# Two transformer blocks on one core: last routing, norm rows, parameter tables and register loads changed together

## The chip, the cores and the metric

One Trainium2 chip, one of its cores. The metric is the device time of one execution in microseconds; the median of 3 runs of the kernel before is 1259.8 us (1259.2 to 1261.1). A profile was taken of one further execution.

## The reference, cut to what matters

Input x is 256 x 1024, float32. The first block is a norm, one projection, dilated attention beside a gated recurrence, an output projection, and 16 experts of which each takes 32 tokens (expert choice). The second block is a projection, three mixers, a layer norm (`ln1`), a router with 4 groups of 8 experts, and 32 small experts; each token goes to 2 experts of its best group; another layer norm (`ln2`) ends it:

```python
for l in range(DEPTH):
    h = hybrid_mixer(x, w_in[l], ...)
    x = layer_norm(DEEPNORM_ALPHA * x + h, ln1_w[l], ln1_b[l])
    h = hier_moe(x, router_group_w[l], router_group_b[l], router_expert_w[l], router_expert_b[l], ...)
    x = layer_norm(DEEPNORM_ALPHA * x + h, ln2_w[l], ln2_b[l])
```

The experts of the first block hold 192 MB of weights, those of the second 96 MB; each is read once.

## The kernel before, in words

**Stages.** `block1_mix` (first mixers), `moe1_route` and `moe1_experts` (first experts), the second block's mixers (`s5_mix`, `moba_mix`, `rwkv_mix`, `merge`), `mix_out` (output projection, layer norm, router logits), `moe2_route` and `moe2_experts` (second experts), `moe2_overflow` (a branch that is taken only when an expert has more tokens than its places), `finish` (last norm and stores). Rows of tokens come in two halves of 128, called a = 0 and 1.

**Order.** The engines take their instructions in order, each from its own queue; a planner fixes the order of each queue at build time from its own estimates, within the data dependences. `issue_after(ins)` adds a rule of order only: what the block emits on the engine of `ins` is queued behind `ins`. Loads are issued by SyncE (`nc.sync`), a few by ScalarE (`nc.scalar`) and GpSimd (`nc.gpsimd`); an issuing engine waits in its queue until the load's buffer is free.

**Weight loads of the second experts.** `prefetch2` issues loads of 1 MB in the order `ORDER2` (for each group of four experts gate and up of each, then the four downs; before the last group an extra set `E2` of weights, picked by a register that holds the number of the fullest expert, L1730). The buffers are a first-in first-out list `k.free2` of 18: six of `ringg`, five of `ey` and `x2p`, three of `ring`, one each of `X` (which holds x3 until then) and `cp2` (which holds the tables), two of `ringh`. A product that has used its weights appends their buffers to the list. Each of the 16 double steps of `moe2_experts` (L2002 gate and up of two experts, L2037 down of four) waits for its loads. In its last but one round of four experts, three buffers leave the list for good (`restore3`): two for norm rows, one for the rows `k.pre`.

**Routing.** `norm_rows` brings a half of x3 to SBUF, transposes it and takes the statistics; `logits` makes the router's 36 numbers per token; `split_rows` normalises the half (VectorE, L1637), and splits it into a high part (ScalarE, L1639, reading with a stride of 8 elements) and a low part (GpSimd, L1640). `route` (L1780 to L1789) picks the experts on VectorE in ten small operations; `moe2_route` counts places by a matmul (L1815, L1817), forms the one-hot `oh` of the first 8 experts (L1819), gathers their tokens by matmul (L1823) and evacuates them into `xi` (L1760 on ScalarE, L1762 on VectorE). `weights2` then makes the weights, the number of the fullest expert (`xid`) and the overflow flag (`over`, L1859); `onehot` makes the next octets' one-hots (L1959) and, on GpSimd, the weighted ones (L1961). `over` is loaded into a register of every engine (L1871).

**Norm rows and tables.** `load_norm` (L2102) reads each of the four vectors ln1_w, ln1_b, ln2_w, ln2_b from memory 128 times, into all partitions, on GpSimd's queue. `setup2` and `load_s5` load three parameter tables (L759, L760, L766) on ScalarE's queue between the first block's experts 3 and 4; `fold_router` (L1675 to L1687) uses them on GpSimd, then TensorE (L1683).

## Time and profile before

| | us |
|---|---|
| median of 3 runs | 1259.8 |
| profiled execution | 1256.34 |
| its span | 1254.6 |
| TensorE busy | 1039.7 |
| VectorE busy | 517.4 |
| ScalarE busy | 370.3 |
| GpSimd busy | 135.4 |

The span runs from the first to the last instruction of the profiled execution; the profiled execution's own time is slightly longer. PE is TensorE, PEld its weight loads, DVE VectorE, ACT ScalarE, POOL GpSimd, SP SyncE; SPq is SyncE's queue of instructions that issue loads. An engine's busy time does not say that it sets the end.

### The profile page before, as it was taken

The numbers are of one execution on the slowest core, as the hardware profiler recorded it, in microseconds if no ns is written. First come the engines' busy times: TensorE is split into PE (matmuls) and PEld (weight loads), VectorE is DVE, ScalarE is ACT, GpSimd is POOL, SyncE is SP. The second block draws the span as 40 slices with busy tenths as digits, with TensorE's granted clock in tenths as the row PEclk, the third lists the DMA queues.
The fourth block names the chain that finished last, engine by engine and source line by source line (L and its number), as shares of the span: only waits on it lengthen the run. The fifth ranks groups of instructions, "written<-read, shape, count | busy, mean of one in ns | idle before, by whom it ended". The sixth has DMA issues, their size and how long they took to land. (4 is left out here: it accounts for less than half of the span.)

```text
span 1254.6 us, 21023 instructions
## 1 busy us (share of the span) xinstructions
PE 1039.7 (83%) x8986; PEld 718.3 (57%) x8986; DVE 517.4 (41%) x1034; ACT 370.3 (30%) x634; POOL 135.4 (11%) x134
## 2 busy tenths in 40 slices
PE   8889997777668777767689999999999979666775
PEld 7889874344214233312169998898999855333332
DVE  5595653102374000124047564686638552111114
ACT  5445632100000000200034565843433532111112
POOL 1351000010060000000001100112002210004101
PEclk9999998988779889987899999998999989888778
DMA  9723579999999999999973342242146659999994
GB/s 365 288 83 116 203 289 365 379 402 407 421 420 421 420 421 420 421 420 421 420 303 133 135 168 101 101 168 103 61 178 248 261 227 419 421 420 420 419 421 165
DMA packets 52949, 375.58 MB, mean 299 GB/s; under 512 B 5874, under 2 KB 6130, under 8 KB 8051
## 3 DMA queue, kind: packets, MB, share of 16 engines
q1 hardware_dynamic: 51842, 370.09, 73.6%
q10 hardware_dynamic: 432, 2.00, 0.5%
q0 software_dynamic: 576, 2.10, 0.4%
q8 instruction: 72, 1.18, 0.4%
q14 instruction: 27, 0.21, 0.0%
HBM read 373.12 MB, written 1.05 MB: 298 GB/s over the span
## 5 line engine op out<-in xcount | busy, mean ns | idle before, releaser
L692 PE MATMUL mx<-w,xin 128*32 128x512 f32 x1024 | 180.6, 662 | 61.3 <-DMA w<-in_w_expert_up_dram 45.9
L776 DVE TENSOR_TENSOR wl<-w,wh 128x1024 fp32r<-128x1024 f32 x116 | 148.3, 1281 | 76.0 <-ACT wh L775 75.6
L775 ACT CAST wh<-w 128x1024 fp32r<-128x1024 f32 x118 | 123.3, 1048 | 112.9 <-PE pj L793 63.6
L793 PE MATMUL pj<-x,wh 128*128 128x256 f32 x800 | 152.4, 289 | 1.2 <-ACT wh L775 0.7
L692 PEld LDWEIGHTS mx<-w,xin 128*32 128x32 f32 x1024 | 37.0, 115 | 181.0 <-DMA w<-in_w_expert_up_dram 82.5
L793 PEld LDWEIGHTS pj<-x,wh 128*128 128x128 f32 x800 | 126.4, 193 | 5.1 <-issue 2.3
L793 PE MATMUL pj<-x,wl 128*128 128x256 f32 x400 | 114.7, 287 | 0.2
L2002 PE MATMUL mx<-w,xi 128*32 128x256 f32 x1024 | 76.6, 404 | 38.4 <-DMA w<-in_expert_w_gate_dram 36.0
L719 PE MATMUL mx<-w,hT 128*32 128x256 f32 x1024 | 81.5, 472 | 17.4 <-DMA w<-in_w_expert_down_dram 9.2
L704 ACT ACTIVATE sg<-mx,rsl 64x512 f32<-64x512 f32 x16 | 10.9, 682 | 239.4 <-PE mx L692 237.2
L793 PEld LDWEIGHTS pj<-x,wl 128*128 128x128 f32 x400 | 77.3, 193 | 1.1 <-DVE wl L776 0.6
L2002 PEld LDWEIGHTS mx<-w,xi 128*32 128x32 f32 x1024 | 36.6, 115 | 70.6 <-issue 48.0
L705 DVE SCALAR_TENSOR_TENSOR sg<-sg,rsl,mx 64x512 f32<-64x512 f32 x16 | 12.0, 749 | 145.5 <-ACT sg L704 145.4
L719 PEld LDWEIGHTS mx<-w,hT 128*32 128x32 f32 x1024 | 37.9, 132 | 54.1 <-issue 20.6
L727 DVE COPY ysb<-mx 32x256 f32<-32x256 f32 x32 | 13.5, 423 | 112.4 <-ACT ysb L727 112.4
L807 PE MATMUL pj<-wh,hT 128*128 128x256 f32 x320 | 57.6, 281 | 0.0
L727 ACT COPY ysb<-mx 32x256 f32<-32x256 f32 x32 | 11.6, 362 | 141.5 <-PE mx L719 134.3
L807 PEld LDWEIGHTS pj<-wh,hT 128*128 128x128 f32 x320 | 49.1, 189 | 1.0 <-ACT osq L447 0.3
L2037 PE MATMUL mx<-w,hT 128*32 128x512 f32 x264 | 44.9, 633 | 0.5 <-ACT hT L2017 0.5
L807 PE MATMUL pj<-wl,hT 128*128 128x256 f32 x160 | 44.7, 279 | 0.0
L1704 DVE TENSOR_TENSOR sg<-sg,mx 64x256 f32<-64x256 f32 (+1 forms) x17 | 7.2, 423 | 87.9 <-ACT sg L1703 87.9
L1545 PE MATMUL mx<-y,wh 128*128 128x256 f32 x192 | 36.2, 288 | 1.5 <-DVE y L825 1.3
(606 smaller groups left out, 1836.8 us busy)
## 6 DMA issues: line engine op xcount, KB each, us to landing
w<-in_w_expert_gate_dram SPq DMA_DIRECT2D x64, 1024.0 KB, 14.9
w<-in_w_expert_up_dram SPq DMA_DIRECT2D x64, 1024.0 KB, 13.2
w<-in_w_expert_down_dram SPq DMA_DIRECT2D x64, 1024.0 KB, 13.7
w<-in_w_in_dram SPq DMA_DIRECT2D x43, 1024.0 KB, 5.0
w<-in_expert_w_gate_dram SPq DMA_DIRECT2D x33, 1024.0 KB, 19.9
w<-in_expert_w_up_dram SPq DMA_DIRECT2D x33, 1024.0 KB, 19.8
w<-in_expert_w_down_dram SPq DMA_DIRECT2D x33, 1024.0 KB, 19.8
w<-in_w_out_dram SPq DMA_DIRECT2D x8, 1024.0 KB, 4.8
```

The source lines that it names most:

```text
L692: last = T.matmul(ps1[32 * i:32 * i + 32, :], x, w[:, kk, 512 * (i % 2):512 * (i % 2) + 512], start=(j + kk == 0), stop=(j == 3 and kk == 1))
L704: A.activation(sg, ps1[0:64, :], AF.Silu, scale=k.rsl[:, e:e + 1])
L705: V.scalar_tensor_tensor(sg, sg, k.rsl[:, e:e + 1], ps1[64:128, :], OP.mult, OP.mult)
L719: last = T.matmul(ps3[32 * q:32 * q + 32, 0:256], hT[:, ft % 4, (ft // 4) * 32:(ft // 4) * 32 + 32], d[:, kk, q * 256:(q + 1) * 256], star ...
L727: done = (V.tensor_copy if q % 2 else A.copy)(ysb[r0:r0 + 32, q * 256:(q + 1) * 256], ps3[32 * q:32 * q + 32, 0:256])
L775: k.halved = k.nc.scalar.copy(h, src).ins
L776: eng.tensor_tensor(l, src, h.bitcast(F32), OP.subtract)
L793: T.matmul(ps[:, m * S:(m + 1) * S], u[:, kk, :], v[:, kk, :], start=(kk + i == 0), stop=(kk == 7 and i == 2))
L807: T.matmul(ps[:, a * S:(a + 1) * S], u[:, 4 * kh + kk, a * P:(a + 1) * P], v[:, kk, :], start=(kh + a + kk + i == 0), stop=(kh + a == 2 an ...
L1545: T.matmul(pu[:, m * S:(m + 1) * S], u[:, kk, m * P:(m + 1) * P], v[:, kk, :], start=(kk + n == 0), stop=(kk == 3 and n == 2))
L2002: T.matmul(ps[64 * i + 32 * n:64 * i + 32 * n + 32, 0:256], x, ws[n][i][:, kk, :], start=(kk == 0), stop=(kk == 7))
L2037: T.matmul(py[q][32 * i:32 * i + 32, :], h[:, j, 32 * i:32 * i + 32], w[i][:, j, 512 * q:512 * q + 512], start=(j == 0), stop=(j == 1))
```

## The change

The three tables are issued on GpSimd's queue. `split_rows` writes the normalised half into a tile of its own, in the order that the split reads (VectorE for a = 0, ScalarE for a = 1); ScalarE copies the high part, VectorE takes the low part, for a = 1 behind the last pick. `route(1)` is emitted before `split_rows(1)`. Two counting products are queued behind the last gather on TensorE, `weights2` behind the last one-hot and the next octet's one-hot behind the last evacuation on VectorE. The two register loads are queued on SyncE behind the weight load emitted last before them. The norm vectors are loaded once as 4 rows (`load_norms`, one round of four experts earlier, where three buffers leave the list) and spread over the partitions by a product with a column of the identity and a copy by ScalarE (`spread_norm`).

```diff
--- before.py
+++ after.py
@@ -756,14 +756,14 @@
     n = k.s5o
     both = k.cp2.tile([P, n + k.io["cf2"].shape[1]], F32, tag="w0", bufs=1, name="p2")
     k.p2, k.c2f = both[:, 0:n], both[:, n:]
-    nc.scalar.dma_start(k.p2, k.io["p2"][:, 0:n])
-    nc.scalar.dma_start(k.c2f, k.io["cf2"])
+    nc.gpsimd.dma_start(k.p2, k.io["p2"][:, 0:n])
+    nc.gpsimd.dma_start(k.c2f, k.io["cf2"])
 
 
 def load_s5(k):
     n, m = k.s5o, k.io["p2"].shape[1]
     k.p2s = k.s5t.tile([P, m - n], F32, name="p2s")
-    k.nc.scalar.dma_start(k.p2s, k.io["p2"][:, n:m])
+    k.nc.gpsimd.dma_start(k.p2s, k.io["p2"][:, n:m])
 
 
 def split(k, src, eng=None):
@@ -1602,6 +1602,7 @@
     k.x3h = k.xg.tile([P, 2, D], F32R, name="x3h")
     k.x3l = k.xg.tile([P, 2, D], F32R, name="x3l")
     k.x3T = k.xg.tile([P, 8, S], F32, tag="xi2", bufs=2, name="x3T")
+    k.x3w = k.xg.tile([P, 2, D], F32, tag="xi2", bufs=2, name="x3w")
     k.lg = k.xg.tile([P, 2, 36], F32, name="lg")
     rw = k.p2v("rw").rearrange("p (k n) -> p k n", k=8)
 
@@ -1633,11 +1634,17 @@
         V.scalar_tensor_tensor(lg, lg, st[:, 4:5], k.rcs[:, 1], OP.mult, OP.add)
 
     def split_rows(a, st):
-        x = k.x3[:, a, :]
-        V.tensor_scalar(x, x, st[:, 1:2], st[:, 4:5], OP.add, OP.mult)
+        x, hi, lo = k.x3[:, a, :], k.x3h[:, a, :], k.x3l[:, a, :]
+        whole = k.x3w[:, a, :]
+        if a:
+            V.tensor_tensor(st[:, 7:8], st[:, 1:2], st[:, 4:5], OP.mult)
+            A.activation(by_row(whole), turned(x), AF.Identity, bias=st[:, 7:8], scale=st[:, 4:5])
+        else:
+            V.tensor_scalar(by_row(whole), turned(x), st[:, 1:2], st[:, 4:5], OP.add, OP.mult)
         with k.tc.issue_after(k.rows3.ins):
-            A.copy(by_row(k.x3h[:, a, :]), turned(x))
-        return G.tensor_tensor(by_row(k.x3l[:, a, :]), turned(x), by_row(k.x3h[:, a, :]).bitcast(F32), OP.subtract)
+            A.copy(hi, whole)
+        with k.tc.issue_after(k.picks2[a].ins) if a else nullcontext():
+            V.tensor_tensor(lo, whole, hi.bitcast(F32), OP.subtract)
 
     for m in range(8):
         if m == 4:
@@ -1657,13 +1664,13 @@
     out_rows(7, 1)
     logits(0, st[0])
     norm_rows(1, st[1])
+    route = route_rows(k)
     split_rows(0, st[0])
-    route = route_rows(k)
     route(0)
     with k.tc.issue_after(k.picks2[0].ins):
         logits(1, st[1])
+    route(1)
     split_rows(1, st[1])
-    route(1)
 
 
 def fold_router(k):
@@ -1727,10 +1734,11 @@
         src = k.io[f"expert_w_{name}_2"].rearrange("e (p k) n -> e p k n", p=P)
         if e == E2:
             if name == "gate":
-                k.more2 = k.nc.values_load(k.xid[0:1, 0:1], engines=(mybir.EngineType.SP,), min_val=0, max_val=E2 - 1)
+                with k.tc.issue_after(k.loads2.ins):
+                    k.more2 = k.nc.values_load(k.xid[0:1, 0:1], engines=(mybir.EngineType.SP,), min_val=0, max_val=E2 - 1)
             k.nc.sync.dma_start(t, src[bass.ds(k.more2, 1)].rearrange("e p k n -> p (e k) n"))
         else:
-            k.nc.sync.dma_start(t, src[e])
+            k.loads2 = k.nc.sync.dma_start(t, src[e])
 
 
 def loaded2(k, e, *names):
@@ -1759,7 +1767,7 @@
     if kk % 2:
         k.nc.scalar.activation(xi[:, kk, :], ps, AF.Identity, scale=w, bias=b)
     else:
-        k.nc.vector.tensor_scalar(xi[:, kk, :], ps, w, b, OP.mult, OP.add)
+        return k.nc.vector.tensor_scalar(xi[:, kk, :], ps, w, b, OP.mult, OP.add)
 
 
 def route_rows(k):
@@ -1816,18 +1824,19 @@
         if a:
             T.matmul(ps[:, 0:32], one, mk[:, 0, :], start=False, stop=True)
         V.tensor_tensor(k.pos[:, a], ps[:, 0:32], mk[:, a], OP.mult)
-        V.tensor_tensor(oh[:, a], io32(k), k.pos[:, a, 0:8, None].to_broadcast([P, 8, C2]), OP.is_equal)
+        k.last_oh = V.tensor_tensor(oh[:, a], io32(k), k.pos[:, a, 0:8, None].to_broadcast([P, 8, C2]), OP.is_equal)
         for kk in range(8):
             sl = slice((kk % 2) * 256, (kk % 2 + 1) * 256)
             for x in (k.x3h, k.x3l):
-                T.matmul(pg[kk // 2][:, sl], x[:, a, kk * P:(kk + 1) * P], oh[:, a].rearrange("p e c -> p (e c)"),
+                last = T.matmul(pg[kk // 2][:, sl], x[:, a, kk * P:(kk + 1) * P], oh[:, a].rearrange("p e c -> p (e c)"),
                          start=(a + kk % 2 == 0 and x is k.x3h), stop=(a == 1 and x is k.x3l), skip_group_check=True)
             if a:
-                gathered2(k, xi, kk, pg[kk // 2][:, sl])
+                k.last_xi = gathered2(k, xi, kk, pg[kk // 2][:, sl]) or k.last_xi
     k.wt2 = Wt.rearrange("p a g e -> p a (g e)")
     ps = k.pj()
-    T.matmul(ps[:, 0:32], one, mk[:, 0, :], start=True, stop=False)
-    T.matmul(ps[:, 0:32], one, mk[:, 1, :], start=False, stop=True)
+    with k.tc.issue_after(last.ins):
+        T.matmul(ps[:, 0:32], one, mk[:, 0, :], start=True, stop=False)
+        T.matmul(ps[:, 0:32], one, mk[:, 1, :], start=False, stop=True)
 
     def weights():
         ge, gs, ng, nm, w2, ex, rd, hw = (t(n, nm) for n, nm in ((4, "ge"), (1, "gs"), (1, "ng"), (1, "nm"), (1, "w2"), (8, "ex"), (1, "rd"), (8, "hw")))
@@ -1868,7 +1877,8 @@
     V, A, G, T = nc.vector, nc.scalar, nc.gpsimd, nc.tensor
     ident = k.c1("ident")
     ln = k.ln1
-    over = nc.values_load(k.over[0:1, 0:1], min_val=0, max_val=1)
+    with tc.issue_after(k.loads2.ins):
+        over = nc.values_load(k.over[0:1, 0:1], min_val=0, max_val=1)
     wg, wu = (k.io[n].rearrange("e (p k) n -> e p k n", p=P) for n in ("expert_w_gate_2", "expert_w_up_2"))
     wd = k.io["expert_w_down_2"].rearrange("e (p k) n -> e p k n", p=P)
     k.rone = pool.tile([P, 1], F32, name="rone")
@@ -2053,12 +2063,14 @@
                     T.matmul(acc[a][q], o[:, a * P:(a + 1) * P], y[:, 512 * q:512 * q + 512],
                              start=(g == 0 and y is yy[g][0]), stop=(g == NQ - 1 and y is yy[g][1]))
 
-    k.weights2()
+    with k.tc.issue_after(k.last_oh.ins):
+        k.weights2()
     onehot(0)
     for g in range(NQ):
         o = g // 2
         if g % 2 == 0 and o + 1 < NQ // 2:
-            onehot(o + 1)
+            with k.tc.issue_after(k.last_xi.ins):
+                onehot(o + 1)
         if g == NQ - 1:
             gate_up("x")
         gate_up(2 * g)
@@ -2077,6 +2089,8 @@
         gate_up(2 * g + 1)
         if o + 1 < NQ // 2:
             gather(o + 1, 2 * (g % 2) + 1)
+        if g == NQ - 3:
+            load_norms(k)
         if g == NQ - 2:
             gather_more()
             restore3(k)
@@ -2094,22 +2108,31 @@
                                    accum_out=k.st2[a][:, 5 + q:6 + q])
 
 
-def load_norm(k, slot, n):
+def load_norms(k):
+
+    k.last2 = [k.free2.pop(0) for _ in range(3)]
+    k.lnr = k.slot_tile(*k.last2[1], (4, D))
+    k.nc.gpsimd.dma_start(k.lnr, k.io["lnv"])
+
+
+def spread_norm(k, slot, n):
 
     t = k.slot_tile(*slot, (P, 2, D))
-    src = k.io["lnv"]
     for i in range(2):
-        k.nc.gpsimd.dma_start(t[:, i, :], bass.AP(tensor=src.tensor, offset=src.offset + (2 * n + i) * D, ap=[[0, P], [1, D]]))
+        row = k.c1("ident")[0:4, 2 * n + i:2 * n + i + 1].to_broadcast([4, P])
+        for q in range(2):
+            sl = slice(512 * q, 512 * q + 512)
+            ps = k.mx()
+            k.nc.tensor.matmul(ps, row, k.lnr[:, sl], start=True, stop=True)
+            k.nc.scalar.copy(t[:, i, sl], ps)
     return t
 
 
 def restore3(k):
 
     G = k.nc.gpsimd
-    k.last2 = [k.free2.pop(0) for _ in range(3)]
-    ln = load_norm(k, k.last2[0], 0)
+    ln, k.lnv2 = (spread_norm(k, k.last2[2 * n], n) for n in range(2))
     k.pre = x = k.slot_tile(*k.last2[1], (P, 2, D))
-    k.lnv2 = load_norm(k, k.last2[2], 1)
     for a in range(2):
         G.tensor_tensor(turned(x[:, a, :]), by_row(k.x3h[:, a, :]).bitcast(F32), by_row(k.x3l[:, a, :]).bitcast(F32), OP.add)
         G.tensor_tensor(x[:, a, :], x[:, a, :], ln[:, 0, :], OP.mult)
```

## Rows read from the trace of the kernel before

**Rows 1.** Stretches: bounds, length, busy PE PEld DVE ACT POOL, clock, DMA share, GB/s.
```profile
246.00:251.00 5.00, 4.56 (x69) 2.34 (x70) 0.51 (x2) 0.36 (x1) 0.20 (x1) 1.00 0.53 171
350.00:640.00 290.00, 207.44 (x1559) 81.00 (x1552) 69.72 (x182) 26.25 (x56) 16.03 (x25) 0.89 1.01 421
640.00:1004.00 364.00, 355.03 (x3501) 331.04 (x3499) 226.20 (x327) 183.71 (x293) 44.49 (x35) 0.99 0.43 155
1020.00:1024.50 4.50, 4.50 (x69) 2.68 (x62) 1.91 (x10) 2.82 (x5) 0.55 (x1) 1.00 0.08 31
1030.00:1230.00 200.00, 150.32 (x1343) 74.38 (x1345) 29.99 (x59) 30.51 (x70) 20.65 (x18) 0.85 1.01 420
```
**Rows 2.** Timeline of TensorE's weight loads, 1235 to 1237: start, us, what, [idle before, releaser].
```profile
1235.84 0.18 PEld L2037 LDWEIGHTS mx<-w,hT 128*32 128x32 f32 x5 [0.25 <-DMA w<-in_expert_w_down_dram]
```
**Rows 3.** Waits of SyncE's queue, 1014.8 to 1023.5: total us, times, longest.
```profile
SPq L1871 <- DVE over L1859: 3.2, 1, 3.2
```
**Rows 4.** The same waits, 1023.5 to 1024.1.
```profile
SPq L1733 <- PE mx L2002: 0.6, 1, 0.6
```
**Rows 5.** Timeline of SyncE's queue, the 18th and the 19th load.
```profile
1014.54 0.33 SPq L1733 DMA_DIRECT2D w<-in_expert_w_up_dram  x1
1023.79 0.33 SPq L1733 DMA_DIRECT2D w<-in_expert_w_gate_dram  x1
```
**Rows 6.** Timeline of all engines, 987 to 1025, the routing and the first product.
```profile
987.25 1.05 ACT L775 CAST wh<-w 128x1024 fp32r<-128x1024 f32 x1 [2.04 <-PE mx L1598]
988.34 1.23 DVE L776 TENSOR_TENSOR wl<-w,wh 128x1024 fp32r<-128x1024 f32 x1 [1.49 <-ACT wh L775]
...
999.96 2.06 ACT L1639 CAST x3h<-x 128x1024 fp32r<-128x1024 f32 x1
1002.10 2.85 POOL L1640 TENSOR_TENSOR x3l<-x,x3h 128x1024 fp32r<-128x1024 f32 x1 [20.38 <-ACT x3h L1639]
1002.10 2.86 DVE L1781 SCALAR_TENSOR_TENSOR r_o<-lg,r_gm,p 128x4 f32<-128x4 f32 x1
...
1007.85 0.81 DVE L1637 TENSOR_SCALAR x<-x,lnst 128x1024 f32<-128x1024 f32 x1
1008.97 0.22 DVE L1781 SCALAR_TENSOR_TENSOR r_o<-lg,r_gm,p 128x4 f32<-128x4 f32 x1
1009.17 0.42 DVE L1959 TENSOR_TENSOR oh<-cf,pos 128x256 fp32r<-128x256 f32 x1
1010.82 1.28 ACT L1837 ACT_TABLE_LOAD   x1
1010.90 2.86 DVE L1788 TENSOR_TENSOR r_hm<-r_rp,r_es 128x8 f32<-128x8 f32 x1
1015.32 0.41 DVE L1819 TENSOR_TENSOR oh<-cf,pos 128x256 fp32r<-128x256 f32 x1
1020.90 3.22 PE L2002 MATMUL mx<-w,xi 128*32 128x256 f32 x54
```
**Rows 7.** Loads by line: count, KB each, median us from issue to landing.
```profile
w<-in_expert_w_gate_dram SPq DMA_DIRECT2D x33, 1024.0 KB, 19.9
w<-in_lnv_dram POOLq DMA_DIRECT2D x4, 512.0 KB, 9.9
```
**Rows 8.** Load queues of the page: packets, MB, share of 16 engines' span.
```profile
q0 software_dynamic: 576, 2.10, 0.4%
```
**Rows 9.** Instructions on the weight tiles, 1205 to 1235: ns min/median/max.
```profile
L2037 PE MATMUL mx<-w,hT x41: 592/592/617, 1210.7 to 1235.0; 128*32 128x512 f32 x41
```
**Rows 10.** Timeline of TensorE, 1160 to 1202.
```profile
1167.60 1.03 PE L2002 MATMUL mx<-w,xi 128*32 128x256 f32 x2 [10.16 <-DMA w<-in_expert_w_gate_dram]
...
1201.16 1.03 PE L2002 MATMUL mx<-w,xix 128*32 128x256 f32 x2 [6.29 <-DMA w<-in_expert_w_gate_dram]
```
**Rows 11.** Waits of SyncE's queue, 237.3 to 253.
```profile
SPq L184 <- DMA p<-in_p_dram: 15.7, 1, 15.7
```
**Rows 12.** Timeline of TensorE, 282 to 292.
```profile
285.99 1.87 PE L1683 MATMUL mx<-p,ones 128*128 128x36 f32 x16
```

## Prediction

> **What bounds the kernel now.** I read the stages first, in the table of stretches [rows 1]. The reader is to see three regimes. Up to 640 us, and again from 1030 to 1230 us, the 16 DMA engines show a share of 1.01 and 420 GB/s: expert weights stream and every other engine waits for them. From 640 to 1004 us TensorE is busy 355 of 364 us and nothing else matters. Between 1020 and 1024.5 us the DMA share is 0.08: the stream of the second experts stands still. Next I asked whether the end hangs on that stream. It does: the last down product waits 0.25 us for its weights at 1235.84 us, and from there a fixed tail runs [rows 2]. So whatever idles the DMA engines in the two streaming stages, or adds bytes there, comes back at the end one for one, as long as TensorE keeps up; what happens between 640 and 1004 us only shifts.
>
> Then I looked at why the stream stands still at 1020. SyncE's queue holds two register loads, of which the second waits 3.2 us for `over` [rows 3]; that looks like the culprit. But the weight load behind them waits a further 0.6 us, for a matmul of the first gate-and-up product [rows 4]. The timeline of that queue says why: 18 weight loads of the second experts have been issued up to 1014.54 us, which is every one of the 18 buffers, and the 19th, at 1023.79 us, can only go when that product frees a buffer [rows 5]. The restart is thus set by the chain from the last routing to the end of the first product, 1020.90 + 3.22 = 1024.12 us [rows 6].
>
> **The change part by part.** *Shorter routing.* In that chain two tiny VectorE instructions, L1781 and L1788, last 2.86 us each, exactly beside the two 2.85 us subtractions of GpSimd at L1640; the same L1781 with GpSimd idle takes 0.22 [rows 6]. With the subtraction on VectorE both stretches go: 2 x (2.86 - 0.22) = 5.3 us. The 0.81 us normalisation of the second half (L1637) moves to ScalarE, for one small product of about 0.2: 0.6 gained. The one-hot of the next octet (0.42, L1959) and some three small operations of the weights (0.17 each, an estimate from the 0.22 row) now queue behind the last one-hot and the evacuations: 0.9 gained. VectorE gets the two subtractions, 1.23 each by the contiguous L776. The first can delay the first routing and is counted whole; the second is placed behind the last pick and lies partly beside the counting matmuls: half, 0.6. Sum 5.3 + 0.6 + 0.9 - 1.23 - 0.6 = 4.9 us. ScalarE's share is two passes for the second half, 2.06 (strided, L1639) and 1.05 (contiguous, L775); it runs beside the routing of that half, and what is late next is the low part, about when the one-hot is. Bounds: the stretch from the last one-hot (1015.32 + 0.41) to 1024.12 is 8.4 us and I leave it as it is. It can lose: the table load of 1.28 us and the exponentials behind it ran at 1010.8 us, ahead of that stretch, and now fall into it, between evacuations, for up to 3 us, and the second subtraction may count whole; then 1.3 is left. It can win: the first subtraction may find a gap (1.2), and the stretch holds 64 products at 3.22/54 = 0.06 us, four side by side on the array, and 16 gathers of full width, at four times that by estimate: 3.8 + 3.8 = 7.6 of the 8.4; then 4.9 + 1.2 + 0.8 = 6.9. Two counting products for the overflow test also move behind the gathers; I take nothing for them.
>
> *Register loads behind the weight loads.* Alone they are worth 0.6 at most, since the load behind them waited for TensorE anyway [rows 4]. They become necessary: with the chain 4.9 us shorter, a queue still stuck on `over` would hold the restart. Their new places are between two weight loads and behind the last; the queue issues one load per 2.5 us (1024 KB at 420 GB/s) and runs 19.9 us ahead of the landing [rows 7], so a microsecond there is covered. Behind the last load only the stores of the result queue, much later. I take 0.
>
> *Norm rows.* Four loads of 512 KB on GpSimd's queue spread the two norms over the partitions; that queue is 0.4% of 16 engines over the span, 0.004 x 1254.6 = 5.0 us (4.4 to 5.6 by the rounding) [rows 7, 8]. They run while the stream is saturated, so they cost their time in full. One load of 16 KB replaces them: gain 5.0. TensorE gets 8 products of 512 columns at 0.59 us as in L2037, 4.7 us [rows 9], and ScalarE 8 copies. The cover is TensorE's waiting for weights, single waits of 10.16 and 6.29 us in this stage [rows 10]; without it the 4.7 would return. Three buffers also leave the ring one group of experts earlier; the queue's 19.9 us of lead covers waits for the remaining 15. On GpSimd's queue the one load may wait for its buffer, and behind it stand the scatter weights of the last octet (L1961), which only the last two groups read.
>
> *Parameter tables.* One weight load on SyncE waited 15.7 us, until the table `p2` issued by ScalarE had landed [rows 11]. In 246 to 251 us the DMA share is 0.53, so 5 x 0.47 = 2.35 us of stream are lost [rows 1]. I read it as a completion counter that both queues' loads share; GpSimd's loads have others. Its weight loads then no longer wait, buffers permitting: I take 2.35. Bounds: 0 if the buffer was the true cause, 2.7 if a small dip later goes too. The tables' first user on TensorE is at 285.99 us, 33 us after the landing at 252.9 [rows 12]; that hides any slowness of the new queue, and GpSimd's own folding, which waits for the same table, has no earlier reader. The trace shows VectorE busy 0.51 of these 5 us [rows 1]. The Trainium skill (SBUF — State Buffer, "SBUF: two separate sides") warns that a load issued on GpSimd starves for descriptors while VectorE holds the port pair that the two share, and advises ScalarE's or SyncE's queue, against this edit. By that rule the tables come later and the sum stays, unless they come after 286 us; no row here shows such a load beside a busy VectorE.
>
> **Sum.** 4.9 + 5.0 + 2.35 = 12.25 us. The profiled execution took 1256.34 us (span 1254.6), so 1244.1 for its like; the median shown is 3.5 above it, 1259.8, so I forecast a median of 1247.5 us.
>
> **Rivals.** (a) *The routing gives back what it gains*: exponentials and their table load sit between the evacuations; 1.3 + 5.0 + 2.35 = 8.65, 1251.2 us. For it: the 1.28 us row; against: they were never needed before the first scatter weights. (b) *More*: 6.9 + 5.0 + 2.7 = 14.6, 1245.2. For it: 8.4 us for 7.6 of products; against: evacuations stand between them, and they stay. (c) *TensorE becomes the bound*: the 8 spreads fall into the last stage where it is busy without a gap, and 4.7 returns: 1252.2. Against: they belong two groups before the end. (d) *Slower, by starvation*: TensorE takes its work in order; if the spreads stand early and their 16 KB load must first wait for its buffer, at worst a group of 12 loads at 2.5 us and a landing of 9.9 us [rows 7], TensorE stands 40 us and frees nothing. Beyond the 19.9 us of lead every microsecond starves the stream: 20 lost, 1267.5. It turns the sum negative from a stand of about 32 us. Against: the loads of 512 KB found buffers at once. The late tables belong to this side too: past 286 us they cost one for one, from 298 us the whole gain. (e) *It does not do what it says*: the planner orders everything anew and the chain and waits stay; within 0.2% of 1259.8.
>
> **How the numbers follow.** Forecast 0.50 (its own range 1245 to 1250), (a) 0.16, (b) 0.14, (c) 0.10, (d) 0.05, (e) 0.05. 0.2% is 2.5 us, about what a measurement here can tell from no change: faster 0.90, same 0.05, slower 0.05. The range 1243 to 1255 takes in (a), (b) and (c) with their bounds and leaves out (d), (e) and some of the tails.
>
> **What would show it.** Routing: L1781 and L1788 near 0.2 us, the first gate-and-up product ending near 1017 (4.9 plus the tables' 2.35 earlier), and a weight load issued just then with no register load ahead. Norms: no 512 KB loads, eight small products that do not end a wait of the stream, DMA share 1.01 from the restart to the last weights. Tables: share near 1.0 in 246 to 251. The forecast is wrong if that share falls below 0.95 anywhere in the last stage, if TensorE's waits for weights vanish there, or if the first product still ends above 1020.

## The result, and the profile after

The changed kernel takes 1243.97 us (median of 6 runs, 1239.98 to 1248.26); the kernel before, beside it, 1259.5 (6 runs, 1254.74 to 1261.11). The ratio is 0.9885, 95% interval [0.9853, 0.9918]; it is estimated from the single runs, here as below, and need not be the quotient of the two medians. Forecast were 1247.5 and a gain of 12.25; measured is 15.5 between the medians and 15.0 between the two profiled executions (1256.34 and 1241.34; spans 1254.6 and 1239.6).

Stretches of the changed kernel (columns as in [rows 1]):
```profile
246.00:251.00 5.00, 3.29 (x37) 1.96 (x41) 1.17 (x2) 0.35 (x1) 0.00 (x0) 0.83 1.01 421
350.00:640.00 290.00, 201.71 (x1568) 81.06 (x1569) 67.44 (x168) 27.78 (x59) 12.93 (x17) 0.92 1.01 420
1010.00:1013.00 3.00, 3.00 (x54) 1.89 (x56) 2.45 (x17) 2.85 (x8) 0.61 (x1) 1.00 0.02 5
1020.00:1215.00 195.00, 158.40 (x1376) 77.05 (x1370) 29.69 (x58) 35.36 (x79) 18.84 (x15) 0.86 1.01 420
```
Both streaming stages of [rows 1] are there. The hole at 246 to 251 (share 0.53) has gone, the stand before the restart remains (0.02), and the last stage streams without a gap.

The routing and the first product, timelines of VectorE, ScalarE, SyncE's queue and TensorE (start, us, what, [idle before, releaser]; line numbers are those of the kernel that ran, so a line of the kernel before has another number here):
```profile
996.24 1.21 DVE L1647 TENSOR_TENSOR x3l<-x3w,x3h 128x1024 fp32r<-128x1024 f32 x1
997.38 0.21 DVE L1789 SCALAR_TENSOR_TENSOR r_o<-lg,r_gm,p 128x4 f32<-128x4 f32 x1
...
1002.42 0.17 DVE L1796 TENSOR_TENSOR r_hm<-r_rp,r_es 128x8 f32<-128x8 f32 x1
...
1002.78 1.22 DVE L1647 TENSOR_TENSOR x3l<-x3w,x3h 128x1024 fp32r<-128x1024 f32 x1
1004.57 0.19 DVE L1826 TENSOR_TENSOR pos<-pj,Mk 128x32 f32<-128x32 f32 x1 [0.56 <-PE pj L1825]
1004.79 0.42 DVE L1827 TENSOR_TENSOR oh<-cf,pos 128x256 fp32r<-128x256 f32 x1
...
1007.70 0.75 DVE L1969 TENSOR_TENSOR oh<-cf,pos 128x256 fp32r<-128x256 f32 x2
```
```profile
1001.93 1.28 ACT L1846 ACT_TABLE_LOAD   x1
```
```profile
1004.34 0.33 SPq L1741 DMA_DIRECT2D w<-in_expert_w_up_dram  x1
1013.11 0.33 SPq L1741 DMA_DIRECT2D w<-in_expert_w_gate_dram  x1
```
```profile
994.79 1.07 PE L1621 MATMUL mx<-cf,x 128*128 128x128 f32 x8
...
1005.36 0.35 PE L1831 MATMUL mx<-oh,x3h 128*128 128x256 f32 x1 [0.83 <-DVE r_nm L1844]
...
1010.23 3.22 PE L2012 MATMUL mx<-w,xi 128*32 128x256 f32 x54
```
The two stretched instructions of [rows 6] (2.86 us each) last 0.21 and 0.17. The product's row ends at 1013.45; the restart is issued just ahead of that, at 1013.11, 10.68 us earlier than in [rows 5]. The wait ahead of it is for TensorE alone, with no register load (waits of SyncE's queue, 1003 to 1024: total, times, longest):
```profile
SPq L1741 <- PE mx L2012: 11.7, 2, 8.4
SPq L1741 <- PE pj L1825: 3.2, 1, 3.2
```
The norm rows: on GpSimd's queue one load of 16 KB stands in place of the four of 512 KB (count, KB each, us to landing). The spreads on TensorE, with its last wait for weights ahead of them, run inside the streaming stage:
```profile
w<-in_lnv_dram POOLq DMA_DIRECT2D x1, 16.0 KB, 5.3
```
```profile
1153.79 1.03 PE L2012 MATMUL mx<-w,xi 128*32 128x256 f32 x2 [8.02 <-DMA w<-in_expert_w_gate_dram]
...
1170.15 6.51 PE L2126 MATMUL mx<-w,cf 4*128 4x512 f32 x8
...
1177.59 7.19 PE L2126 MATMUL mx<-w,cf 4*128 4x512 f32 x8
```
The last weights are awaited at 1219.83 us where they were at 1235.84 [rows 2]:
```profile
1219.83 0.17 PEld L2047 LDWEIGHTS mx<-w,hT 128*32 128x32 f32 x5 [0.26 <-DMA w<-in_expert_w_down_dram]
```

To split the 15.0 us I followed the weight stream itself: the bytes of SyncE's queue, summed packet by packet over the trace, are the same in every kernel (370.09 MB, a MB being a million bytes), so the time between two marks compares stages alone. Three intervals carry the change: from the 64th to the 82nd MB (tables), from the second transposes of the rows (L1620 before, L1621 after) to the restart (routing), and from the 330th to the 350th MB (norm rows).
```
times in us                   64-82 MB   transposes-restart   330-350 MB
before                          53.12         23.26             52.79
after                           49.41         18.32             47.70
e1 tables                       49.45         23.29             52.84
e2 norms                        56.85         23.30             47.73
e3 routing                      52.91         18.34             52.84
e4 registers                    53.84         24.44             52.85
e5 all but registers            49.34         19.20             47.74
e6 first product last           48.13         19.27             47.68
e7 remainder on GpSimd          50.86         21.24             47.77
e8 one table                    52.07         23.26             52.81
e9 busy through routing         49.69         19.13             47.63
e10 busy and product last       49.43         16.85             47.69
```
How far executions with the same code in an interval differ says what these numbers can bear: up to 4 us for the tables (52.91 to 56.85 in before, e2, e3 and e4; 48.13 to 50.86 with all tables on GpSimd's queue), about 1 us for the routing, 0.15 us for the norm rows.

The routing interval splits at the start of the gather of the second half. Beside it stands for how long TensorE's granted clock was at 0.5 (1.2 GHz) in that interval, rounded:
```
times in us                   transposes-gather   gather-restart   at half clock
before (e1, e2, e8 alike)           15.35              7.91             10
after                               10.57              7.75              3.5
e3 routing                          10.59              7.75              3.5
e4 registers                        15.95              8.49             14
e5 all but registers                11.45              7.75              7
e6 first product last               11.23              8.04             10
e7 remainder on GpSimd              12.07              9.17             10
e9 busy through routing              9.92              9.21              3.5
e10 busy and product last            9.92              6.93              0
```
Between the two profiled executions: tables 3.71, routing 4.94, norm rows 5.09, together 13.7. Of the rest, 0.5 was lost ahead of the first mark, 0.5 came at 626 to 672 us and 2.0 to 2.2 at 820 to 864, where the change touches nothing, and 0.7 went again in the tail.

### The profile page after: what moved, and what is told of

Read it like the earlier page. It is cut to its first block, busy times and chain, and to the rows that moved or that the text cites. A ratio compares the mean times of both kernels' runs of the same rounds, so it can differ in the third digit from the quotient of the medians.

```text
span 1239.6 us, 21063 instructions
## 1 busy us (share of the span) xinstructions
PE 1037.2 (84%) x9002; PEld 717.4 (58%) x9002; DVE 514.2 (41%) x1036; ACT 375.1 (30%) x643; POOL 128.1 (10%) x132
## 3 DMA queue, kind: packets, MB, share of 16 engines
q1 hardware_dynamic: 51842, 370.09, 74.6%
HBM read 371.04 MB, written 1.05 MB: 300 GB/s over the span
## 5 line engine op out<-in xcount | busy, mean ns | idle before, releaser
L692 PE MATMUL mx<-w,xin 128*32 128x512 f32 x1024 | 176.2, 645 | 61.4 <-DMA w<-in_w_expert_up_dram 45.1
L2012 PE MATMUL mx<-w,xi 128*32 128x256 f32 x1024 | 75.4, 399 | 33.3 <-DMA w<-in_expert_w_gate_dram 33.3
## 6 DMA issues: line engine op xcount, KB each, us to landing
w<-in_w_expert_down_dram SPq DMA_DIRECT2D x64, 1024.0 KB, 13.7
w<-in_expert_w_up_dram SPq DMA_DIRECT2D x33, 1024.0 KB, 19.8
w<-in_expert_w_down_dram SPq DMA_DIRECT2D x33, 1024.0 KB, 19.8
```

The source lines that it names most:

```text
L692: last = T.matmul(ps1[32 * i:32 * i + 32, :], x, w[:, kk, 512 * (i % 2):512 * (i % 2) + 512], start=(j + kk == 0), stop=(j == 3 and kk == 1))
L2012: T.matmul(ps[64 * i + 32 * n:64 * i + 32 * n + 32, 0:256], x, ws[n][i][:, kk, :], start=(kk == 0), stop=(kk == 7))
```

## The experiments

**One part at a time.** Each of the first four is the kernel before with one part of the diff. e1, tables alone:
```diff
-    nc.scalar.dma_start(k.p2, k.io["p2"][:, 0:n])
-    nc.scalar.dma_start(k.c2f, k.io["cf2"])
+    nc.gpsimd.dma_start(k.p2, k.io["p2"][:, 0:n])
+    nc.gpsimd.dma_start(k.c2f, k.io["cf2"])
...
-    k.nc.scalar.dma_start(k.p2s, k.io["p2"][:, n:m])
+    k.nc.gpsimd.dma_start(k.p2s, k.io["p2"][:, n:m])
```


> The kernel before with the table loads alone moved from ScalarE's queue to GpSimd's. In the trace after, the weight stream stands 2.4 us earlier from 290 us on and 3.3 us earlier from 300 us on, against 0.4 us later at 240 us. Theory: the 15.7 us wait of a weight load for a table's landing goes, and with it the stream's gap in 246 to 251; the stream is 3.5 us earlier at 600 us (3.0 to 4.0) and the time 1256 where before has 1259.5 (ratio 0.997). Rival 1, the size of the forecast: 2.4 us, the 0.9 us won at 293 being an accident of that execution. Rival 2: the restart of the stream after the routing does not follow the earlier start, because matrix products of the routing stage set it: 0.

1254.69 us beside 1260.22, ratio 0.9943 [0.9917, 0.9969]. The interval took 49.45 us, as in the full change, and the routing (23.29) and the last 20 MB (52.84) kept their lengths: the theory holds and rival 2 falls; that the forecast's 2.35 was too small rests on all the executions together (below), since one pair can be off by more than the difference. Waits of SyncE's queue, 237 to 262 us, in e1:
```profile
SPq L184 <- DMA w<-in_w_expert_up_dram: 12.1, 1, 12.1
SPq L184 <- DMA w<-in_w_expert_down_dram: 4.3, 2, 2.2
```
The 15.7 us for a table of [rows 11] is gone; what is left are waits for weights of the stream itself.

e2, norm rows alone (`load_norms`, `spread_norm` and the call two groups before the end):
```diff
-    ln = load_norm(k, k.last2[0], 0)
+    ln, k.lnv2 = (spread_norm(k, k.last2[2 * n], n) for n in range(2))
     k.pre = x = k.slot_tile(*k.last2[1], (P, 2, D))
-    k.lnv2 = load_norm(k, k.last2[2], 1)
```


> The kernel before with the norm rows alone changed: one load of 16 KB and 8 spreads by TensorE in place of four loads of 512 KB. Theory: 2 MB less on a stream at share 1.01 give 5.0 us between the restart and the last landing, and nothing before: time 1254.5 against 1259.5 (ratio 0.996); the last landing and the end both move by 5.0. Rival 1: the end is set by TensorE and the tail, so that the stream ends 5.0 earlier and the end moves under 2. Rival 2: the gain in the trace after at 1145 to 1190 came from another order of loads behind the shorter routing, and alone the edit gives 2.5 or less.

1253.73 us, ratio 0.994 [0.9917, 0.9964]. The last 20 MB took 47.73 instead of 52.79: 5.06 us, with nothing gained ahead of it. Both rivals fall.

e3, routing alone:
```diff
-        return G.tensor_tensor(by_row(k.x3l[:, a, :]), turned(x), by_row(k.x3h[:, a, :]).bitcast(F32), OP.subtract)
+        with k.tc.issue_after(k.picks2[a].ins) if a else nullcontext():
+            V.tensor_tensor(lo, whole, hi.bitcast(F32), OP.subtract)
...
+    with k.tc.issue_after(k.last_oh.ins):
+        k.weights2()
```


> The kernel before with the routing's edits alone; the two register loads stay ahead of the weight loads on SyncE. Theory, as forecast: the chain is 4.9 us shorter by itself, but the register loads of before ended 0.6 us ahead of the restart at 1023.79, so that left where they are they hold the restart at about 1023: 0.6 to 1 us gained, time 1258.7, and the weight loads wait behind a register load. Rival: what the registers are read from comes earlier with the chain, the register loads move with it, and the restart comes 4.9 us earlier: time 1254.6 (ratio 0.996), and the register edit is worth nothing in any company.

1252.55 us, ratio 0.9929 [0.99, 0.9959]. Transposes to restart: 18.34, the 18.32 of the full change, with the register loads where they were. The rival is right. Waits of SyncE's queue, 1003 to 1024 us:
```profile
SPq L1737 <- DVE r_rd L1849: 6.7, 1, 6.7
...
SPq L1740 <- PE mx L2010: 1.3, 1, 1.3
```
The register load came earlier with the chain, and the weight load behind it still waited 1.3 us for TensorE.

e4, the register loads alone:
```diff
-    over = nc.values_load(k.over[0:1, 0:1], min_val=0, max_val=1)
+    with tc.issue_after(k.loads2.ins):
+        over = nc.values_load(k.over[0:1, 0:1], min_val=0, max_val=1)
```


> The kernel before with the two register loads alone put behind the weight loads. Theory: the restart is set by the first gate-and-up product, which frees the buffers, so the time stays at 1259.5 within 0.6 us (ratio 1.000), with the restart at 1023.2 to 1023.8. Rival: the register loads on SyncE hold the first load back by the time that they take, and the restart and the end come 1 us or more earlier.

1258.92 us, ratio 0.9993 [0.997, 1.0016]: nothing that can be measured. The restart came 24.44 us after the transposes, 1.2 later than before, and not at the 1023.2 to 1023.8 expected. The clock rows of the kernel before and of this execution, over the same stretch from the transposes on, bear on that (columns as above, the clock is the third from the end):
```profile
1005.20:1020.20 15.00, 9.82 (x48) 7.61 (x48) 12.91 (x53) 5.92 (x12) 3.76 (x3) 0.66 0.41 151
```
```profile
1006.00:1021.00 15.00, 9.83 (x39) 8.29 (x40) 12.05 (x50) 5.38 (x11) 3.02 (x2) 0.58 0.43 164
```
TensorE stood at half clock for 14 us and not 10, and 0.6 us of the 1.2 lie on either side of the second gather's start. That the clock explains all of it is argued, not shown.

**All but the register loads.** e5 is the changed kernel with both `issue_after(k.loads2.ins)` taken back (e4's diff reversed).

> The changed kernel with the two register loads back ahead of SyncE's weight loads. Forecast: with the chain 4.9 us shorter the register loads, that ended 0.6 us before the restart, become what holds the first weight load, so the time between the second transposes of the rows and the restart goes from 18.32 us (the changed kernel) to 22 to 23, and the time from 1244 to 1248. Rival, from the routing alone, where it was 18.34 with the register loads unmoved: 18.2 to 18.5, and the time of the changed kernel within 0.6 us.

1244.99 us, ratio 0.9898 [0.9875, 0.992]; the full change's 0.9885 lies inside. 19.20 us is 0.9 over both the changed kernel and e3, far from the forecast's 22. The queue's register wait was over in time (1003 to 1030 us; weight loads waited for TensorE behind it):
```profile
SPq L1740 <- PE mx L2010: 8.4, 3, 3.7
SPq L1737 <- DVE r_rd L1849: 6.9, 1, 6.9
```
Here TensorE ran at half its clock through the whole first gather (0.51 in 1002 to 1008), for 7 us and not 3.5. The trace places all of the 0.9 there: up to the second gather it is 11.45 against 10.57, behind it 7.75 in both. In the changed kernel already, VectorE waits 0.56 us for the counting product (L1825), which stands behind the first gather in TensorE's queue, so a slower first gather delays the restart.

**What stretched the routing.** e7 puts the remainder of the changed kernel back on GpSimd:
```diff
-        with k.tc.issue_after(k.picks2[a].ins) if a else nullcontext():
-            V.tensor_tensor(lo, whole, hi.bitcast(F32), OP.subtract)
+        G.tensor_tensor(lo, whole, hi.bitcast(F32), OP.subtract)
```


> The changed kernel with one thing undone: the remainder of the split (x minus its rounded part) computed by GpSimd again, from the same contiguous rows. Theory: while GpSimd runs it, one small VectorE operation of the routing stretches from 0.2 to over 2 us, once in each half: plus 5.3, less the 1.2 us of VectorE that go and 0.6 of the second; from the second transposes to the restart 21.8 us (20.5 to 22.5) where the changed kernel has 18.3, and the time 3.5 us over it. Rival: what stretched those operations was the strided reading of the rows, not GpSimd's running; then VectorE is freed of 1.2 to 1.8 us and the stretch is 16.5 to 17.3.

1247.19 us, ratio 0.9908 [0.9883, 0.9933]; 21.24 us, inside the theory's bounds, but not for its reasons. Timelines of GpSimd and of VectorE, and TensorE's clock:
```profile
1001.52 2.42 POOL L1646 TENSOR_TENSOR x3l<-x3w,x3h 128x1024 fp32r<-128x1024 f32 x1 [19.33 <-ACT x3h L1645]
1010.28 2.35 POOL L1646 TENSOR_TENSOR x3l<-x3w,x3h 128x1024 fp32r<-128x1024 f32 x1 [6.34 <-ACT x3h L1645]
```
```profile
1001.77 0.68 DVE L1622 COPY x3T<-mx 128x512 f32<-128x512 f32 x1
1002.36 0.15 DVE L1787 TENSOR_REDUCE r_gm<-lg 128x1 f32<-128x4 f32 x1
1002.55 1.42 DVE L1788 SCALAR_TENSOR_TENSOR r_o<-lg,r_gm,p 128x4 f32<-128x4 f32 x1
...
1011.90 1.00 DVE L1826 TENSOR_TENSOR oh<-cf,pos 128x256 fp32r<-128x256 f32 x1
```
```profile
1006.50:1016.70 10.20, 8.13 (x33) 6.99 (x34) 6.41 (x25) 5.60 (x6) 2.35 (x1) 0.50 0.60 222
```
L1788 ends at 1003.97, as GpSimd's subtraction does (1003.94): 1.42 us for 0.21, on contiguous rows. So GpSimd's running does hold VectorE, and the rival falls by this row. But the mix is not the one expected. The last pick ended 8.33 us after the transposes, only 0.25 later than in the changed kernel (8.08; 13.51 before), since the 1.2 that the hold cost came in place of VectorE's own subtraction. In the second half GpSimd began at 1010.28, behind the last pick (1009.31), and held the one-hot for 0.6 us instead of a routing step for 2.7. The other 2.1 of the 2.9 us over the changed kernel go with TensorE at half clock for 10 us instead of 3.5: 0.7 ahead of the second gather, whose counting products stand behind the slow first gather, and 1.4 behind it. That the sum fell inside the theory's bounds is chance.

**One table left on ScalarE's queue.** e8 is the kernel before with this alone:
```diff
-    nc.scalar.dma_start(k.p2, k.io["p2"][:, 0:n])
+    nc.gpsimd.dma_start(k.p2, k.io["p2"][:, 0:n])
     nc.scalar.dma_start(k.c2f, k.io["cf2"])
```


> The kernel before with only the first and larger of the tables (727 KB) moved to GpSimd's queue; the second (679 KB) stays on ScalarE's and still waits for TensorE until 248.4. Theory, one landing counter for each load, shared by the loads of SyncE and ScalarE: the weight load eight loads on waits for the second table's landing instead, some 15 us as before, and the stream gains nothing at 300 us (0, up to 0.8 for the bytes that go elsewhere): time 1259 to 1260. Rival, that the gap came from the tables' bytes or from the queue that carries them: half of them gone gives half the 3.7 us, with a wait of 8 us or less.

1257.81 us beside 1258.43, ratio 0.9986 [0.9969, 1.0002]. Waits of SyncE's queue, 237 to 262 us:
```profile
SPq L184 <- DMA p<-in_cf_dram: 17.6, 1, 17.6
```
The wait stays whole and only changes its table; one table on ScalarE's queue is enough to stop SyncE's. The semaphores in the traces (counters that an instruction can wait for) show why. The loads of SyncE and ScalarE count their landings on eight semaphores in turn. Before, table `p2` counts on number 109; SyncE waits for 109 until 252.88 us, where its last count has come at 252.87, and the next weight load counts on 109 too. Here it is the second table that counts on 109, and SyncE waits for it until 257.89. In the changed kernel the tables count on 111 to 113, and no weight load does. So the shared counter is shown, and it was not the weight load's buffer. The interval was 1.05 us shorter than before, a little over the 0.8 allowed; with the spread of this interval that can't be told from nothing.

**A shorter way to the restart.** In the trace after, ScalarE's four evacuations of the gather follow each other at 0.98 us, because three single products of the first gate-and-up, 0.55 us each, stand between the gather's pairs. e6 puts that product behind the last gather:
```diff
-        gate_up(2 * g)
+        with nullcontext() if g else k.tc.issue_after(k.last_gather.ins):
+            gate_up(2 * g)
```


> The changed kernel with the first gate-and-up product put behind the last gather product on TensorE. In the trace after, three single products of 0.55 us each stand between the gather's last pairs, at 1006.91, 1007.89 and 1008.88, and ScalarE's evacuations follow each other at 0.98 us instead of 0.5. Theory: those 1.65 us come off the chain, the last evacuation ends at 1009 and not at 1010.5, the product at 1011.7 and not at 1013.4, and the restart and the end come 1.3 to 1.7 us earlier (time 1242.4 where the changed kernel has 1244). Rival: evacuations by VectorE and ScalarE set the pace, the products only fill gaps, and standing behind them they end later: restart 0.5 to 2 us later.

1245.06 us, ratio 0.988 [0.9856, 0.9904]; 19.27 us, 0.95 more than the changed kernel. The evacuations did close up (1.93 us for four), but the clock was granted at 1.2 GHz through both gathers:
```profile
1003.00:1013.00 10.00, 8.42 (x39) 8.32 (x39) 7.06 (x25) 5.03 (x9) 0.00 (x0) 0.51 0.64 215
```
A product of the second gather took 0.21 us instead of 0.12. In the changed kernel the clock was low from 1000 to 1003.5 only. e9 (the changed kernel) and e10 (e6) therefore keep TensorE at work in the thin stretch ahead, with products whose results are thrown away:
```diff
+    def keep_busy(n, after):
+        with k.tc.issue_after(after.ins):
+            for _ in range(n):
+                m = T.matmul(pg[3], k.x3h[:, 0, 0:P], k.x3h[:, 0, 0:512], start=True, stop=True, skip_group_check=True)
+        return m
+
+    done = keep_busy(5, k.last_logit)
     for a in range(2):
         ps = k.pj()
-        T.matmul(ps[:, 0:32], tri, mk[:, a, :], start=True, stop=(a == 0))
+        with k.tc.issue_after(done.ins):
+            done = T.matmul(ps[:, 0:32], tri, mk[:, a, :], start=True, stop=(a == 0))
+        if a == 0:
+            done = keep_busy(3, done)
```


> The changed kernel with eight products of 128x512 added on TensorE whose results are thrown away: five behind the second half's logits and three behind the first counting product, in the 2.4 us in which TensorE does nearly nothing (998.3 to 1000.7 in the trace after), before the granted clock falls to 1.2 GHz. Theory: the clock stays at 2.4 GHz through the gather of the first half (0.12 us a product and not 0.21), which does not set the restart in the changed kernel, since VectorE's routing of the second half ends later; from the second transposes to the restart 18.0 to 18.4 us, no change in the time. Rival: the added products stand in the way of the counting product, 0.3 to 1 us later.

> The same eight products, and the first gate-and-up product behind the last gather product. Put behind alone, it made ScalarE's four evacuations follow each other at 0.48 us, as expected, but TensorE ran at 1.2 GHz until 1013 in that execution, so that the second gather took 0.21 us a product and the restart came no earlier. Theory: with the clock kept up, the second gather takes 0.12 us a product and the restart follows the second transposes after 16.2 to 16.8 us (18.3 in the changed kernel), time 1242. Rival: the order alone costs as much as it gains, whatever the clock: 18.0 us or more.

e9: 1243.45 us beside 1260.84, ratio 0.9865 [0.9829, 0.99], and 19.13 us from transposes to restart, outside what the theory allowed. The clock held through the first gather and fell in the second (columns as above):
```profile
998.00:1012.00 14.00, 12.32 (x86) 10.42 (x85) 10.84 (x42) 10.03 (x17) 0.00 (x0) 1.00 0.64 217
1013.50:1016.50 3.00, 3.00 (x13) 0.97 (x11) 1.58 (x5) 1.13 (x2) 0.00 (x0) 0.50 0.50 205
```
e10: 1241.39 us, ratio 0.9872 [0.9831, 0.9914], and 16.85 us, 1.47 less than the changed kernel and just above the range expected, with the clock at full level throughout and the evacuations closed up:
```profile
998.00:1014.00 16.00, 14.77 (x138) 11.06 (x142) 14.03 (x63) 11.33 (x21) 1.23 (x2) 1.00 0.61 226
```
```profile
1006.40 0.35 PE L1841 MATMUL mx<-oh,x3h 128*128 128x256 f32 x1 [1.15 <-DVE r_nm L1855]
```
```profile
1008.05 1.93 ACT L1768 ACTIVATE xi<-mx,ln 128x256 f32<-128x256 f32 x4 [1.29 <-PE mx L1841]
```
The 1.47 us are two things. In e9 and e10 alike the second gather starts 9.92 us after the transposes, 0.65 earlier than in the changed kernel: with the first gather at full clock the counting product is no longer awaited. So the clock of the first half does count, against what e9's theory said. Behind that start e10 takes 6.93 us and the changed kernel 7.75, both at full clock: the order is worth 0.8 us, half of what e6's theory promised. One execution of each shows it; the timed runs can't separate e10 from the changed kernel. The clock was up through the first gather in both executions with the added products and down in all five of the changed routing without them (after, e3, e5, e6, e7); since e9's fell later all the same, that the products kept e10's up to the end is not shown.

## Why the prediction was right, and where it was not

**What bounds the kernel**: right. What was won in the two streaming stages came back at the end, term by term: each edit alone moved its own interval by what it moved in company (49.45 and 49.41, 18.34 and 18.32, 47.73 and 47.70), closer for the first two than their spread would let one expect. No engine took over. The tail that the forecast called fixed is not: from TensorE's last wait for weights to the end of the span it is 18.7 us before and 19.8 after, and 19.8 in e1 too, which has the code of before there.

**Routing, 4.9 forecast**: 4.94 measured (the terms as written add up to 4.97). That it agrees to better than the 1 us by which executions differ is luck. The two instructions lost 2.65 and 2.69 us against the 5.3 written down, but "with the subtraction on VectorE both stretches go" names the wrong part of the change for most of that. In e7 GpSimd subtracts again, and the last pick still comes 5.18 of the 5.43 us earlier. In the first half ScalarE's copy of contiguous rows takes 1.04 us and not 2.06 and GpSimd's subtraction 2.42 and not 2.85, so less of it falls on the held step. In the second half ScalarE normalises and `route(1)` comes first, so the picks are through before GpSimd starts. GpSimd's running held VectorE; it was the rows and the order that moved most of it off the picks; which of them did how much is read from the timelines and was not tested one by one.

From the transposes to the end of the last one-hot it is 15.20 before and 10.42 after; the stretch behind it, left as it was in the forecast, went from 8.06 to 7.90, though before TensorE ran 3.4 us of it at half clock and after it ran at full clock throughout. The table load that rival (a) put into that stretch ran at 1001.93, ahead of it. The second subtraction was taken at 0.6 for itself; what stands there is VectorE's 0.56 us wait for the counting product behind the first gather at half clock, and in e10, at full clock, the subtraction costs nothing. The forecast has no term for TensorE's clock in the routing. The split between the other small terms (L1637, L1959, the first subtraction) is shown only by the sum.

The Trainium skill (SBUF — State Buffer, "SBUF: two separate sides") says that VectorE and GpSimd share a pair of ports as a lock, also for VectorE operations with two inputs in SBUF against a GpSimd operation that reads it. The traces agree: of the instructions of e7 above, those with two such inputs (L1788, L1826) are long, while the copy from PSUM and the one-input reduction beside the same subtraction took 0.68 and 0.15 us.

**Register loads**: worth 0, as forecast, but the reason given failed. "They become necessary" is refuted by e3: what the register is read from moves with the chain. The 0.6 that it was allowed alone doesn't show in e4.

**Norm rows, 5.0 forecast**: 5.09 in the full change, 5.06 alone. The spreads' price was mis-sized, without harm: 8 products at 0.59 us, 4.7, were forecast, and they held TensorE for 6.51 and 7.19 us, 13.7, with a granted clock of 0.53 from 1170 to 1185. The cover held, but it was used up. TensorE's four waits for weights in the last stage (33.3 us in all) end at 1153.79, ahead of the spreads; where it waited 6.29 us at 1201.16 before [rows 10] it waits no more, and the next wait is the 0.26 us for the last weights. So rival (c) came closer than the forecast thought, and how much was left is not shown. Rival (d) did not come: the load of 16 KB landed in 5.3 us.

**Tables, 2.35 forecast**: 3.71 measured (e1: 3.67). This is the term that was mis-sized, in the step "the DMA share is 0.53, so 5 x 0.47 = 2.35 us of stream are lost". The mechanism stood: e8 and the semaphores show that a table on ScalarE's queue holds SyncE's loads until it has landed. But the busy share is not the stream: by the 171 GB/s in the same row of [rows 1] the loss is 5 x (1 - 171/420) = 3.0 us, and it goes on behind 251 us. Stretches of the kernel before:
```profile
248.00:250.00 2.00, 2.00 (x42) 1.22 (x36) 0.00 (x0) 0.00 (x0) 0.20 (x1) 1.00 0.39 66
250.00:252.00 2.00, 2.00 (x17) 1.16 (x12) 0.69 (x2) 0.72 (x2) 0.00 (x0) 1.00 0.88 334
252.00:254.00 2.00, 2.00 (x19) 1.70 (x22) 0.15 (x1) 0.00 (x0) 1.08 (x3) 1.00 0.99 265
```
At 252 to 254 us the engines are 0.99 busy and move 265 GB/s of the usual 420. By bytes the interval lost 5.5 us before: 53.12, less 18 MB of weights and 2.0 of tables at 420 GB/s, 47.6. The same sum after is 1.8. That makes 3.7. It includes the small dip at 292 to 294 (share 0.82, 332 GB/s), which the forecast saw and left in the upper bound of 2.7. Over all executions the interval is 54.2 us on average with the tables on ScalarE's queue (4 executions) and 49.5 with them on GpSimd's (7), so 4.7, with a spread of some 4 us between executions of the same code there. Part of the spread is the table's own: SyncE's wait for it was 15.7 us in before and e3, 17.2 in e4 and 17.9 in e2, whose interval is the longest. The rule brought against this edit (the same section of the Trainium skill) cost nothing: the first table took 9.6 us to land instead of 4.4, and its first reader on TensorE ran at 282.79 us, 3.2 earlier than before, since nothing hung on it. That VectorE starved the load is not what the traces show: in those 9.6 us VectorE ran two copies of 0.4 us, and in e8, with the stream standing until 257.89, the same load took 6.4. That the running stream beside it slowed it is argued.

**The base.** 2.0 to 2.2 us of the 15.0 are not the change. Stretches of the kernel before, and of e4, which changes nothing there:
```profile
840.00:860.00 20.00, 16.93 (x233) 15.22 (x233) 15.04 (x25) 7.29 (x14) 9.46 (x6) 0.83 0.16 54
```
```profile
840.00:860.00 20.00, 16.82 (x253) 14.64 (x251) 15.89 (x27) 8.61 (x15) 9.48 (x6) 0.91 0.22 75
```
The profiled execution of before had the lower clock in a stage that TensorE bounds; from the 250th to the 256th MB it took 43.95 us, the changed kernel 41.76, e4 41.98. The median of 1243.97 lies in the range 1243 to 1255, but below the forecast's own 1245 to 1250 and below rival (b)'s 1245.2, whose routing term of 6.9 did not come. The forecast of 1247.5 missed it by 3.5: 1.4 for the tables by the pair of traces (2.3 by the averages), 0.3 because before itself ran at 1259.5, and 1 to 2 that I can't place. The timed runs of single parts can't help: e1, e2 and e3 came out at 5.5, 6.5 and 7.7 us below the same runs of before, each more than its interval in the trace, with bounds of 3 us on each.

## What to carry to other kernels

Where a stage is bound by its stream, follow the stream's own bytes from mark to mark: it splits a sum of small edits that timed runs blur by 3 us, to 0.15 us where only the stream sets the pace and to 1 to 4 us where other engines do, so run the same code several times before you trust a pair; and the bytes moved tell of gaps that the busy share hides. A load that must wait for its buffer belongs on a queue whose completions the stream's loads do not wait for. A tiny instruction that lasts exactly as long as its neighbour on another engine is the first thing to look for in a chain of small steps. Then undo the remedy alone: here that showed that most of the gain came from the edits beside it.

## What the runs showed that was not expected

In the thin stretch of the routing TensorE's clock is granted at 1.2 GHz for times that differ from one execution to the next: 3.5 us in the changed kernel, 7 in e5, 10 in e6 and e7, 10 in the kernel before, none in e10. It moved the restart by 1 us and more, as much as the edits tried there.
